# Queries and keys of dilations 1 and 4 by seven products, rotated as pairs of heads inside the pair stage

## The chip, the core and the metric

The kernel runs on one core of a Trainium2 chip. The metric is the device time of one execution in microseconds (us); fewer is better. The engines are named as in the profile: PE is TensorE (matmul), PEld its weight load, DVE is VectorE, ACT is ScalarE, POOL is GpSimd, SP is SyncE, which issues nearly all DMAs.

## The reference

A trunk of two layers on x of (1, 1024, 1024) in fp32. Layer 0 mixes with gated DeltaNet heads and short convolutions, layer 1 with HGRN2 heads and dilated sliding-window attention; each layer is followed by a SwiGLU FFN. What the change touches is the first half of layer 1's mixer:

```python
def mixer_cd(h, w_in, lower_bound, norm_g, w_out):
    hq, hf, hi, hg, sq, sk, sv = split_cols(h @ w_in, CD_SPLITS)
    f_gate = lb + (1.0 - lb) * jax.nn.sigmoid(hf)
    k_in = (1.0 - lb) * jax.nn.sigmoid(-hf)
    o_c = hgrn2_recurrence(silu(hq), k_in, hi, log(f_gate))
    sq = rope(sq.reshape(b, t, n_pat, SWA_HEADS, SWA_DH), pos)
    sk = rope(sk.reshape(b, t, n_pat, SWA_HEADS, SWA_DH), pos)
    for p, (window, dilation) in enumerate(SWA_PATTERNS):   # (128,1), (512,4), (2048,16)
        o_p, lse_p = dilated_window_attention(sq[:, :, p], sk[:, :, p], sv[:, :, p], window, dilation)

def rope(x, pos):
    x1, x2 = xf[..., :half], xf[..., half:]                 # lower and upper 64 of a head's 128 columns
    return concatenate([x1 * cos - x2 * sin, x1 * sin + x2 * cos], axis=-1)
```

There are 4 HGRN2 heads and, for each of 3 dilations, 4 attention heads, all 128 wide. `h @ w_in` has 52 column blocks of 128.

## The kernel before, in words

Every fp32 operand is split into a high and a low part (`split`, L100 to L103: a cast on ScalarE, then a subtraction on VectorE), and each product is three matmuls of 128x128 by 128x512 (`mm3`, L126 to L128: L126 to L128 are the lines on which nearly all matmuls stand). The sequence is held transposed, 128 features on the partitions, and in two halves of 512 tokens.

**Seven products.** Where two column blocks g and u of the same input are wanted, the 2x2 product (two column blocks by two halves of tokens) is made by seven products instead of eight. Class `Up` does so for the FFN, its subclass `Pairs` (L729) for pairs of column blocks of layer 1's mixer. A pair is 7 products x 4 blocks of the half contraction x 3 matmuls = 84 matmuls; the plain way is 96. `HEADS` lists the 12 pairs. ("k", p, h) is key and query of attention head h of dilation group p (0: dilation 1, 1: dilation 4, 2: dilation 16); ("f", h) is forget gate and query of HGRN2 head h. Positions in `HEADS` are counted from 0.

`pair` (and `last_pair`) is one window of the stage; the order on PE, DVE, ACT, POOL and SP is that of the code there (`manual_schedule`). In window f, PE makes p1(f), p2(f), row2(f-1), row1(f-1), p6(f), p5(f), p7(f), 12 matmuls each. Beside them the outputs of pair f-1 are finished: at the start `add22` (ACT copies x from PSUM to `c`, DVE adds z to `c`, L797), then `row2` accumulates on the same PSUM bank x and so needs that copy first; `row1` accumulates on z, and so needs DVE's total first. `add11`, `row1` and `add22` give the sums of both column blocks. In the same window the weights of pair f+1 are made: four sums on POOL (`sums`, L302 and L303; `sums_late`, L307 and L308), four splits on ACT and DVE (`part_a` to `part_d`).

What is done with an output depends on its kind. "k" is stored to DRAM (`qk`). The query of "f" is multiplied by its sigmoid (`query`, L820 and L821) and stored. For the forget gate `forget` (L828 to L840) is a generator for both halves at once: clamp on DVE, exponential and +1 on ACT, reciprocal (L836) and product (L838) on DVE, scale and shift on ACT (L840). `step()` puts its next part into the code order, at three places of a window.

**The mixer behind it.** Then come the projections of the values, gates and the rest as plain products (`hgrn_v`, `swa_v`, `hgrn_gates`), between which attention (`local`) and HGRN2 (`chain`) run. After every few matmuls the projections call `tick(cost)`; it adds cost times `rate` to what is due for the two generators and runs their next step when 1 is due. The PE order is that of the code, DVE's is fixed in these steps. Three forms of rotation are there:

- dilation 1 (`turns`, L1939): q and k are loaded from DRAM twice, once with the halves of the partitions exchanged, rotated by three DVE operations (L1935 to L1937) with a table `turn0` loaded at L1948, stored to `final`, and loaded from there by `Attend.load`.
- dilation 4 (`swa_qk`, L1966): q and k of a head are made by plain products, 96 matmuls; ACT exchanges the halves out of PSUM (L1976, L1977, tile `sw`), DVE rotates (L1980, L1981). `query_keys` calls it for each head.
- dilation 16 (`Attend.load`): loaded, exchanged by DMA and rotated when attention of that head is near; the stage of pairs has written these heads in the order of their 16 streams.

Of the kernel before, what the change touches and what calls it, by code (L numbers as in the profile page):

```python
# [54 lines left out]
def hybrid_trunk_kernel(ctx: ExitStack, tc: tile.TileContext, x_t, w_all, w_down, w_ba, vecs, c_f, c_i, c_rope, out):  # L55
# [673 lines left out]
    class Pairs(Up):  # L729

        early = True
        HEADS = (("k", 0, 0), ("k", 0, 1), ("k", 0, 2), ("f", 0), ("k", 2, 0), ("f", 1), ("k", 2, 1), ("f", 2),
                 ("k", 2, 2), ("f", 3), ("k", 2, 3), ("k", 0, 3))

        def __init__(self, left):
            self.left, self.n = left, 0
            n = len(self.HEADS)
            self.qk = {f[1:]: dr.tile([2, P, 2, HT], F32, name=f"qk{i}") for i, f in enumerate(self.HEADS) if f[0] == "k"}
# [5 lines left out]
            self.work, self.kept_f, self.coming = [], {}, {}  # L744

        def src(self, kind, f):
            f = self.HEADS[f]
            if f[0] == "k":
                return w_all[W_AT["cd", (16 if kind == "g" else 28) + f[1] * 4 + f[2]]]
            return w_all[W_AT["cd", (4 if kind == "g" else 0) + f[1]]]  # L750
# [27 lines left out]
        def fresh(self, name="d"):  # L778
            return self.right.tile([P, HT], F32, tag="d", name=name, bufs=4)

        def place(self, f, c):

            if f < 3:
                return c
            return self.scratch("fc") if self.HEADS[f][0] == "f" else self.fresh()

        def streams(self, f, dst, *srcs):

            n = (None, 4, 16)[self.HEADS[f][1]] if self.HEADS[f][0] == "k" else None
            if n is None:  # L790
                return (dst,) + srcs
            return (dst.rearrange("p (r i) -> p i r", r=n),) + tuple(s.rearrange("p (i r) -> p i r", r=n) for s in srcs)

        def total(self, f, i, half, c, y):

            if (self.HEADS[f][0], i) == ("f", 1):
                V.tensor_tensor(c, c, y, op=ADD)  # L797
                return self.query(f, half, c)
            d = self.place(f, c)
            o, a, b = self.streams(f, d, c, y)  # L800
            V.tensor_tensor(o, a, b, op=ADD)
            self.keep(f, i, half, d)

        def keep(self, f, i, half, d):
            kind = self.HEADS[f]
            if kind[0] == "k":
                dst = self.qk[kind[1:]][i]
                if kind[1] == 2 and i == 0:
                    dma(dst.rearrange("p b t -> p (b t)").rearrange("p (s b i) -> p s b i", s=16, b=2)[:, :, half],
                        d.rearrange("p (s i) -> p s i", s=16))  # L810
                else:
                    dma(dst[:, half], d)
                return
            self.kept_f[kind[1], half] = d
            if half:
                self.work.append(self.forget(kind[1]))
# [7 lines left out]
        def forget(self, h):  # L824
            cs = [self.kept_f.pop((h, half)) for half in range(NH)]
            rs = [self.scratch("fr") for _ in cs]
            for c, r in zip(cs, rs):
                V.tensor_scalar(c, c, -44.0, None, op0=MAX)  # L828
                S.activation(r, c, AF.Exp, scale=-1.0)
            yield  # L830
            for c, r in zip(cs, rs):
                S.activation(c, r, AF.Identity, bias=onec[:, 0:1])
            yield
            om, lb = self.omlb[:, h:h + 1], self.lb[:, h:h + 1]
            for half, (c, r) in enumerate(zip(cs, rs)):
                V.reciprocal(c, c)  # L836
                d = self.fresh("kk")
                V.scalar_tensor_tensor(d, r, om, c, op0=MULT, op1=MULT)  # L838
                dma(self.bkq[h, half][1], d)
                S.activation(c, c, AF.Identity, scale=om, bias=lb)  # L840
                dma(self.bkq[h, half][0], c)
                yield
# [1758 lines left out]
```

## Time and profile before

| | us |
|---|---|
| median of 3 runs | 2572.06 (2570.32 to 2573.62) |
| the profiled execution | 2570.22 |
| its span | 2568.4 |
| busy PE | 2544.8 |
| busy DVE | 1666.6 |
| busy ACT | 1034.8 |
| busy POOL | 522.6 |
| granted clock of PE, mean | 0.998 |

The profile's page and the answers of the trace are of that profiled execution. A line of instructions shows the engine, the line of the kernel, the operation, the tiles (out<-in), shapes and counts; L126 is line 126 of the kernel before. In the waits of TensorE a row says which instruction of which engine ended the wait, how long all such waits were, how many, and the longest. The stage of pairs lies from about 1186 to 1376 us of the span, the mixer with attention and HGRN2 from about 1378 to 1845 us.

### The profile page before, as it was taken

To read this page: it belongs to the slowest core of one execution; us is meant where nothing else is said; L and a number is where in the kernel's file an instruction comes from. 1 tells how busy PE (TensorE), PEld (TensorE's weight loads), DVE (VectorE), ACT (ScalarE), POOL (GpSimd) and SP (SyncE) were. 2 spreads that over 40 slices of the span, in tenths; PEclk is the share of its full clock that TensorE was granted. 3 is DMA by queue.
4 is the path that set the end of the run, shared out by engine and by line. 5 is a ranking of instruction groups with operands and counts; after the bars stand their busy time and mean duration, and the time that the engine had idled before them with its cause. 6 is when DMAs were issued, how large, how long until landed. Compare 5 with 4: busy or idle time off the path is not lost.

```text
span 2568.4 us, 37628 instructions
## 1 busy us (share of the span) xinstructions
PE 2544.8 (99%) x14124; PEld 2120.3 (83%) x14124; DVE 1666.6 (65%) x2823; ACT 1034.8 (40%) x1859; POOL 522.6 (20%) x445
## 2 busy tenths in 40 slices
PE   9999999999999999999999999999999999999998
PEld 7788888888888888887888887888878888888887
DVE  7886777585655665567665586665668565666554
ACT  5432123343333344344444455564544333334442
POOL 1110121334343300033330000000033433330001
PEclk9999999999999999999999999999999999999999
DMA  4434446424556688643336676625652455668853
GB/s 136 149 99 156 121 148 214 161 87 164 178 190 205 215 285 298 189 131 132 122 113 223 207 228 181 191 88 172 213 202 87 164 188 184 201 217 282 280 176 122
DMA packets 287447, 456.03 MB, mean 178 GB/s; under 512 B 50176, under 2 KB 142112, under 8 KB 287136
## 3 DMA queue, kind: packets, MB, share of 16 engines
q1 hardware_dynamic: 287264, 453.62, 54.2%
q8 instruction: 111, 1.82, 0.3%
q14 instruction: 72, 0.59, 0.1%
HBM read 311.36 MB, written 142.16 MB: 177 GB/s over the span
## 4 chain that ended last, share of the span: by engine, by line
PE 73%; DVE 6%; DMA 2%; ACT 1%; issue 1%; POOL 0%; SPq 0%; DVEq 0%; ACTq 0%; POOLq 0%
PE psu L126 13%; PE psu L128 13%; PE psu L127 13%; PE psg L126 5%; PE psg L128 5%; PE psg L127 5%; PE psm L128 4%; PE psm L127 4%; PE psm L126 4%; PE psm L2125 1%; DVE h L223 1%; DVE h L592 1%; PE psm L2067 1%; DMA raw<-in_dram 1%; DVE w L289 1%
## 5 line engine op out<-in xcount | busy, mean ns | idle before, releaser
L103 DVE TENSOR_TENSOR w<-raw,w 128x1024 fp32r<-128x1024 f32 (+1 forms) x321 | 383.7, 1197 | 131.3 <-ACT w L102 130.4
L102 ACT CAST w<-raw 128x1024 fp32r<-128x1024 f32 (+1 forms) x321 | 306.9, 958 | 270.1 <-PE psu L128 126.3
L126 PE MATMUL psu<-hnh,w 128*128 128x512 f32 x880 | 350.9, 399 | 2.8 <-ACT sw L1909 2.4
L128 PE MATMUL psu<-hnh,w 128*128 128x512 f32 x880 | 345.1, 392 | 1.0 <-DVE w L103 1.0
L127 PE MATMUL psu<-hnl,w 128*128 128x512 f32 x880 | 344.0, 391 | 0.5 <-DVE hnl L2374 0.5
L128 PEld LDWEIGHTS psu<-hnh,w 128*128 128x128 f32 x880 | 165.6, 188 | 37.9 <-DVE w L103 3.0
L126 PEld LDWEIGHTS psu<-hnh,w 128*128 128x128 f32 x880 | 165.8, 188 | 37.0 <-ACT sw L1909 2.5
L127 PEld LDWEIGHTS psu<-hnl,w 128*128 128x128 f32 x880 | 165.9, 189 | 34.2 <-DVE hnl L2374 1.3
L187 POOL TENSOR_TENSOR acc<-acc,sq 128x512 f32<-128x512 f32 x52 | 79.0, 1520 | 527.1 <-ACT sq L183 527.0
L302 POOL TENSOR_TENSOR ws<-raw 128x512 f32<-128x512 f32 x50 | 72.3, 1446 | 424.0 <-DMA raw<-in_dram 310.5
L103 DVE TENSOR_TENSOR w<-ws,w 128x1024 fp32r<-128x1024 f32 x47 | 60.7, 1292 | 119.6 <-ACT w L102 119.6
L103 DVE TENSOR_TENSOR hidq<-hr,hidq 128x1024 fp32r<-128x1024 f32 x72 | 82.1, 1141 | 81.3 <-ACT hidq L102 81.1
L102 ACT CAST hidq<-hr 128x1024 fp32r<-128x1024 f32 x72 | 70.3, 980 | 106.1 <-DMA hr<-ts 63.2
L126 PE MATMUL psm<-hidq,w 128*128 128x512 f32 x264 | 102.8, 389 | 0.0
L127 PE MATMUL psm<-hidq,w 128*128 128x512 f32 x264 | 102.8, 389 | 0.0
L128 PE MATMUL psm<-hidq,w 128*128 128x512 f32 x264 | 102.8, 389 | 0.0
L126 PE MATMUL psu<-hidq,w 128*128 128x512 f32 (+2 forms) x242 | 90.7, 375 | 0.0
L127 PE MATMUL psu<-hidq,w 128*128 128x512 f32 (+2 forms) x242 | 90.5, 374 | 0.0
L128 PE MATMUL psu<-hidq,w 128*128 128x512 f32 (+2 forms) x242 | 90.5, 374 | 0.0
L126 PE MATMUL psu<-t3h,w 128*128 128x512 f32 x224 | 87.3, 390 | 1.0 <-ACT u L365 1.0
L126 PE MATMUL psu<-t4h,w 128*128 128x512 f32 x224 | 87.5, 391 | 0.6 <-ACT c L372 0.6
L393 POOL TENSOR_TENSOR hid<-hid,c 128x512 f32<-128x512 f32 x44 | 61.7, 1402 | 125.8 <-ACT hid L392 103.4
(499 smaller groups left out, 6509.7 us busy)
## 6 DMA issues: line engine op xcount, KB each, us to landing
raw<-in_dram SPq DMA_DIRECT2D x227, 512.0 KB, 4.0
sd<-in_dram SPq DMA_DIRECT2D x44, 512.0 KB, 4.0
hid<-hid SPq DMA_DIRECT2D x88, 256.0 KB, 2.7
sd<-sd SPq DMA_DIRECT2D x44, 512.0 KB, 3.1
hr<-ts SPq DMA_DIRECT2D x40, 512.0 KB, 4.5
raw<-sd SPq DMA_DIRECT2D x40, 512.0 KB, 4.7
hd<-h SPq DMA_DIRECT2D x48, 256.0 KB, 3.0
h<-hd SPq DMA_DIRECT2D x48, 256.0 KB, 5.7
```

What stands on the lines that cost most here:

```text
L102: S.copy(hi, src)
L103: eng.tensor_tensor(lo, src, hi.bitcast(F32), op=SUB)
L126: T.matmul(o, lh, rh, start=first and i == 0, stop=False, **kw)
L127: T.matmul(o, lh, rl, start=False, stop=False, **kw)
L128: T.matmul(o, ll, rh, start=False, stop=last and i == n - 1, **kw)
L187: (eng or G).tensor_tensor(a, a, q, op=ADD)
L223: V.scalar_tensor_tensor(h, h, vec[:, row + k:row + k + 1], pb, op0=MULT, op1=MULT)
L289: later(lambda: V.tensor_tensor(u[:, 1, c], src[:, c], u[:, 0, c].bitcast(F32), op=SUB))
L302: G.tensor_tensor(s[:, HT:], b[:, :HT], b[:, HT:], op=ADD)
L393: G.tensor_tensor(h, h, self.c22.pop(f), op=MULT)
L592: eng.tensor_tensor(dst, x, y, op=SUB)
L2067: T.matmul(o[:, z], self.block(self.q, j, 1), self.block(self.k, j, m), start=True, stop=True)
```

## The change

The stage of pairs gets four pairs more and another order. A new kind ("r", p, i, m) is q (i = 0) or k (i = 1) of heads 2m and 2m+1 of dilation 1 (p = 0) or 4 (p = 1). The host reorders the weights' columns, so that one column block has the lower halves of the two heads and the other the upper halves: x1 and x2 of the rotation lie on the same partitions of two tiles. The rotation is then done in the stage of pairs, half of the tokens by half (`rope`): with a (lower) and b (upper),

- t1 = a cos on DVE, t2 = b sin and a = a sin on POOL,
- b = b cos, t1 - t2 and a + b on DVE, each result stored to `qk`. For p = 1 the results are written in the order of their 4 streams.

`turn_heads` puts the first line into the code order, `turned` the second. The table `rt` of cosines and sines has one buffer; `table` loads it, 512 KB for each half of a p = 0 pair, 256 KB once for a p = 1 pair. `swa_qk`, `turns`, `final` and `query_keys` are removed. `Attend.load` loads q and k of dilations 1 and 4 from `qk` in four pieces of 64 partitions; those of dilation 16 are now stored in plain order and permuted as they are rotated. `forget` works on one half at a time. The half of a weight tile that `part_d` fills has a tile of its own (`wd`, 2 buffers). The attention order is all heads of dilation 16, then 4, then 1; `swa_v` ticks in finer steps, and the rates are new.

```diff
-        HEADS = (("k", 0, 0), ("k", 0, 1), ("k", 0, 2), ("f", 0), ("k", 2, 0), ("f", 1), ("k", 2, 1), ("f", 2),
-                 ("k", 2, 2), ("f", 3), ("k", 2, 3), ("k", 0, 3))
+        HEADS = (("k", 2, 0), ("k", 2, 1), ("k", 2, 2), ("f", 0), ("r", 1, 0, 0), ("r", 0, 0, 0), ("f", 1),
+                 ("r", 1, 1, 0), ("r", 0, 1, 0), ("f", 2), ("r", 1, 0, 1), ("r", 0, 0, 1), ("f", 3),
+                 ("r", 1, 1, 1), ("r", 0, 1, 1), ("k", 2, 3))
...
+        def table(self, f, half):
+            if f < 3 or self.HEADS[f][0] != "r":
+                return
+            if self.HEADS[f][1] and half:
+                return
+            self.rt = self.right.tile([P, 2, HT], F32, tag="rt", name="rt", bufs=1)
+            if self.HEADS[f][1]:
+                dma(self.rt[:, :, 0:256], c_rope[:, :, T_LEN:T_LEN + 256])
+            else:
+                dma(self.rt, c_rope[:, :, half * HT:(half + 1) * HT])
+
+        def rope(self, f, half):
...
+            p = self.HEADS[f][1]
+            a, b = (self.held.pop((f, i, half)) for i in range(2))
+            t1, t2 = self.fresh(), self.fresh()
...
+            V.tensor_tensor(v(t1), v(a), cos, op=MULT)
+            G.tensor_tensor(v(t2), v(b), sin, op=MULT)
+            G.tensor_tensor(v(a), v(a), sin, op=MULT)
+            yield
+            V.tensor_tensor(v(b), v(b), cos, op=MULT)
...
+            V.tensor_tensor(d1, v(t1), v(t2), op=SUB)
+            dst = self.qk[self.HEADS[f][1:]]
+            dma(dst[0][:, half], o1)
+            V.tensor_tensor(d2, v(a), v(b), op=ADD)
+            dma(dst[1][:, half], o2)
...
-        def forget(self, h):
+        def forget(self, h, half, c):
+            r = self.scratch("fr")
+            V.tensor_scalar(c, c, -44.0, None, op0=MAX)
+            S.activation(r, c, AF.Exp, scale=-1.0)
+            S.activation(c, r, AF.Identity, bias=onec[:, 0:1])
             yield
...
+            V.reciprocal(c, c)
+            d = self.fresh("kk")
+            V.scalar_tensor_tensor(d, r, om, c, op0=MULT, op1=MULT)
+            dma(self.bkq[h, half][1], d)
+            yield
+            S.activation(c, c, AF.Identity, scale=om, bias=lb)
+            dma(self.bkq[h, half][0], c)
+            yield
...
@@ def pair
                 self.part_d(f, self.a)
                 self.fetch(n + 1)
+            self.turned()
+            self.table(f - 1, 0)
             self.step()
             self.p2(f, b21, psm())
...
             self.row2(f - 1, t4)
             self.part_a(n, an)
+            self.turn_heads(f - 1, 0)
             self.sums_late(an, bn, s)
             self.row1(f - 1, b22)
             self.p6(f, t2)
+            self.turned()
+            self.table(f - 1, 1)
             self.step()
             self.p5(f, t1, psg())
             self.part_b(n, s)
             self.part_c(n, bn)
+            self.turn_heads(f - 1, 1)
             self.a = an
             self.step()
             self.p7(f, t3)
...
-            due, rate = [0.0] * 2, [0.0, 0.72]
+            due, rate = [0.0] * 2, [0.0, 1.05]
...
-                ready += [(h, 2, None) for h in range(3)]
-                next(turner)
-                begun.append(1)
+                ready += [(h, p) for p in (2, 1, 0) for h in range(4)]
+                prepare()
...
                 swa_v(2, tick)
-                rate[0] = 0.5
+                rate[:] = .75, 1.0
...
-                query_keys((0,))
-                ready.append((3, 2, None))
+                rate[0] = 1.0
                 swa_v(0, tick)
-                rate[0] = 0.7
-                query_keys((1, 2, 3))
-                ready += [(h, 0, None) for h in (1, 2, 3)]
-                rate[0] = 1.05
+                rate[0] = 1.1
```

How the order of instructions moves is shown at two places. On DVE, before, in the window after that of a forget pair and on into the next: the clamps of both halves stand together, the reciprocals one window later, the first behind the last half split of the pair (`fc` is the forget gate's tile, `kk` what is stored of it, `w` weights, `c` the total that row1 waits for).

```order
L801 TENSOR_TENSOR fc<-u_10416,psg 128x512
L828 TENSOR_SCALAR fc<-fc 128x512 x2
L103 TENSOR_TENSOR w<-ws,w 128x1024
L103 TENSOR_TENSOR w<-raw,w 128x1024
L801 TENSOR_TENSOR d<-c_10606,psg 128x32x16
L103 TENSOR_TENSOR w<-raw,w 128x512
L836 RECIPROCAL fc<-fc 128x512
L838 SCALAR_TENSOR_TENSOR kk<-fr,omlb,fc 128x512
L801 TENSOR_TENSOR fc<-gt,psm 128x512
```

After, in the window of the forget pair at position 6, the rotation of the pair before it (`d<-gt,rt` to `gt<-gt,d`, then the second half's first product `d<-u,rt`) stands among the splits, and clamp, reciprocal and product of the gate's first half behind it (here the gate is in tile `gt`).

```order
L838 TENSOR_TENSOR d<-gt,rt 128x512
L800 TENSOR_TENSOR u_10148<-u_10148,psg 128x512
L842 TENSOR_TENSOR d<-d,rt 128x512
L848 TENSOR_TENSOR d<-d 128x512
L851 TENSOR_TENSOR gt<-gt,d 128x512
L871 TENSOR_SCALAR gt<-gt 128x512
L103 TENSOR_TENSOR w<-ws,w 128x1024
L103 TENSOR_TENSOR w<-raw,w 128x1024
L838 TENSOR_TENSOR d<-u_10148,rt 128x512
L876 RECIPROCAL gt<-gt 128x512
L878 SCALAR_TENSOR_TENSOR kk<-fr,omlb,gt 128x512
L800 TENSOR_TENSOR c_10359<-c_10359,psg 128x512
```

The reciprocal has moved ahead of the total `c`, the last row, and both stand behind the rotation, two of whose operations need results of POOL.

On ACT, the same place before: the exponentials of both halves (`fr`), two weight casts, +1 for both, then the copy `c` that row2 waits for.

```order
L365 COPY u_10002<-psu 128x512
L829 ACTIVATE fr<-fc 128x512 x2
L102 CAST w<-ws 128x1024
L102 CAST w<-raw 128x1024
L832 ACTIVATE fc<-fr,onec 128x512 x2
L856 COPY c_10056<-psu 128x512
L102 CAST w<-raw 128x512
```

After, exponential and +1 of one half stand together, ahead of the two casts and of the copy `c`.

```order
L365 COPY u_10728<-psu 128x512
L872 ACTIVATE fr<-gt 128x512
L873 ACTIVATE gt<-fr,onec 128x512
L102 CAST w<-ws 128x1024
L102 CAST w<-raw 128x1024
L897 COPY c_10794<-psu 128x512
L865 ACTIVATE r<-c_10794 128x512
```

The order of casts and copy is kept; in front of them stand operations that take their input from DVE's clamp, which is behind the rotation.

More of the change, by code (lines that the diff above doesn't have):

```diff
@@ L778, in fresh, with take, part @@
         def fresh(self, name="d"):
[L779 to L792, printed above, removed]
+            return self.right.tile([P, HT], F32, tag="d", name=name, bufs=6)
+        def take(self):
+            return unit()
+        def part(self, f, src, left, right, later=None, u=None):
+            if left or self.right is None:
+                return super().part(f, src, left, right, later, u)
+            u = self.right.tile([P, 2, HT], F32R, tag="wd", name="w", bufs=2)
+            if later:
+                S.copy(u[:, 0], src[:, HT:])
+                later(lambda: V.tensor_tensor(u[:, 1], src[:, HT:], u[:, 0].bitcast(F32), op=SUB))
+            else:
+                split(u[:, 0], u[:, 1], src[:, HT:])
+            self.units[f][right] = tuple(u[:, z].rearrange("p (k c) -> p k c", k=KH) for z in range(2))
         def total(self, f, i, half, c, y):
+            V.tensor_tensor(c, c, y, op=ADD)
             if (self.HEADS[f][0], i) == ("f", 1):
-                V.tensor_tensor(c, c, y, op=ADD)
                 return self.query(f, half, c)
[L799 to L802, printed above, removed]
+            self.keep(f, i, half, c)
         def keep(self, f, i, half, d):
@@ L806, in keep @@
             if kind[0] == "k":
[L807 to L812, printed above, removed]
-                return
-            self.kept_f[kind[1], half] = d
-            if half:
-                self.work.append(self.forget(kind[1]))
+                dma(self.qk[kind[1:]][i][:, half], d)
+            elif kind[0] == "r":
+                self.held[f, i, half] = d
+            else:
+                self.work.append(self.forget(kind[1], half, d))
@@ L2237, in mixer_cd @@
             lead = {}, {}, {}, (6, 7)
-            ready, late, diag, holding, combined, made, ended = [], [], [], [0], [0], [0], set()
+            ready, late, diag, combined, ended = [], [], [], [0], set()
             unit, ahead, valued, whole = [], [], set(), []
             def prepare():
-                if ready and not ahead and len(unit) // 2 + made[0] < 2:
+                if ready and not ahead and len(unit) // 2 < 2:
                     ahead.append(Attend(*ready.pop(0)))
@@ L2259, in local @@
                         prepare()
-                    holding[0] = len(ahead) + bool(now)
                     if now:
@@ L2289, in run @@
                     next(work, None)
-                    if work is hg_chain and begun:
-                        begun[0] += 1
-                        if begun[0] % 2 and made[0] <= len(coming):
-                            next(turner, None)
-            begun, coming = [], []
-            def arrived():
-                made[0] -= 1
-                ready.insert(0, coming.pop(0)[1])
+                    if work is hg_chain and not unit and ahead:
+                        ahead[0].turn(1)
             def tick(cost):
-                if coming:
-                    coming[0][0] -= cost
-                    if coming[0][0] <= 0:
-                        arrived()
                 for i in range(2):
@@ L2316, in mixer_cd @@
             tokens = (0, 1, 2), (3,), (4,), (5, 6, 7)
-            def query_keys(hs):
-                for h in hs:
-                    while len(unit) // 2 + len(ahead) + len(coming) > 1:
-                        run(loc)
-                    made[0] += 1
-                    qk = swa_qk(h, tick)
-                    coming.append([1.5, (h, 1, qk)])
             for i in range(2):
```

185 lines of the change are left out of this document (78 added, 107 removed).

## The prediction

> **What bounds the kernel now.** The page comes first, for the share of each engine; then the windows view, for the price of one matmul and for the load of the two stages that the change touches; then TensorE's waits.
>
> ```profile
> span 2568.4 us, 37628 instructions
> PE 2544.8 (99%) x14124; PEld 2120.3 (83%) x14124; DVE 1666.6 (65%) x2823; ACT 1034.8 (40%) x1859; POOL 522.6 (20%) x445
> ```
>
> TensorE is busy for 99% of the span, so it is the bound, and time goes only with matmuls or with the few places where it waits. The windows view has, for each stretch, the busy us of PE, PEld, DVE, ACT and POOL (with instructions), the granted clock, the DMA share and GB/s.
>
> ```profile
> 700.00:800.00 100.00, 100.00 (x442) 82.80 (x442) 57.39 (x80) 33.30 (x47) 35.47 (x27) 1.00 0.58 197
> 1206.00:1376.00 170.00, 168.95 (x748) 139.56 (x747) 111.58 (x96) 69.81 (x100) 49.38 (x31) 1.00 0.40 125
> 1378.00:1845.00 467.00, 461.37 (x4267) 394.31 (x4266) 299.18 (x902) 240.93 (x688) 9.99 (x11) 1.00 0.60 185
> ```
>
> The first row is pure products: 100.00 / 442 = 0.226 us for a 128x512 matmul. The second is the stage of pairs, the third the mixer behind it. In both PE has hardly a gap, VectorE (DVE) is 64 to 66% busy, and GpSimd (POOL) works in the first alone. The waits of TensorE that lie in these stages:
>
> ```profile
> PE psu L126 <- ACT sw L1909: 2.4, 1, 2.4
> PE psu L126 <- DVE k L1981: 2.1, 1, 2.1
> PE psu L126 <- ACT u L365: 1.0, 1, 1.0
> ```
>
> **Matmuls.** `swa_qk` made q and k of a dilation-4 head by 96 matmuls; its four heads are 384, all removed. Four more pairs of 7 x 4 x 3 = 84 come in, 336. So 48 fewer: 48 x 0.226 = **-10.8 us**, all on the engine that bounds. It is the one certain term.
>
> **Waits that leave with their code.** The 2.1 us belongs to `swa_qk` and goes. The 1.0 us came where the gate's work of the last forget pair (position 9, counted from 0) still ran in the last pair, position 11; the last forget pair is now at 12, the last at 15: **-3.1 us** together. The 2.4 us (a weight cast that heads ScalarE's queue while its load lands) stands in a stage whose order is new; I keep it as it is, between -4 if it goes and 0. The 4 is worked out from the clock behind it:
>
> ```profile
> 1550.00:1551.00 1.00, 0.66 (x2) 0.57 (x3) 0.93 (x4) 0.97 (x3) 0.00 (x0) 0.52 0.00 0
> 1551.00:1552.00 1.00, 1.00 (x4) 0.80 (x3) 0.08 (x1) 1.00 (x5) 0.00 (x0) 0.50 0.84 315
> 1552.00:1553.00 1.00, 1.00 (x3) 0.77 (x3) 0.46 (x1) 1.00 (x2) 0.00 (x0) 0.50 1.03 375
> 1553.00:1554.00 1.00, 1.00 (x5) 0.76 (x4) 1.00 (x2) 0.04 (x1) 0.00 (x0) 0.77 1.02 199
> 1584.00:1586.00 2.00, 1.48 (x7) 1.20 (x8) 0.38 (x1) 0.00 (x0) 0.00 (x0) 1.00 0.52 176
> ```
>
> Behind the 2.4 us the granted clock is 0.50 to 0.52 for three us and 0.77 in the fourth: (0.48 + 0.50 + 0.50 + 0.23) = about 1.7 us lost beside the wait. Behind the 2.1 us (1584 to 1586) it stays 1.00. So a long wait of TensorE costs itself and about 1.7 us more, a short one only itself.
>
> **Rotation in the pairs.** One pair lasts 84 x 0.226 = 19.0 us, a product 2.71. A rotated pair adds 8 VectorE and 4 GpSimd operations, against 4 sums on GpSimd now. All read two SBUF operands, and there the trace shows that VectorE and GpSimd do not run side by side. One line, two kinds of operand, then a place where it can be watched (start, duration):
>
> ```profile
> L821 DVE SCALAR_TENSOR_TENSOR d<-r,c x4: 801/1780/1784, 1222.4 to 1337.4; 128x512 f32<-128x512 f32 x4
> L821 DVE SCALAR_TENSOR_TENSOR d<-r,psu x4: 686/688/689, 1229.2 to 1343.4; 128x512 f32<-128x512 f32 x4
> ```
>
> ```profile
> 1257.60 1.23 DVE L103 TENSOR_TENSOR w<-ws,w 128x1024 fp32r<-128x1024 f32 x1 [1.82 <-ACT w L102]
> 1261.25 1.78 DVE L821 SCALAR_TENSOR_TENSOR d<-r,c 128x512 f32<-128x512 f32 x1 [0.70 <-ACT r L820]
> 1262.96 1.77 DVE L103 TENSOR_TENSOR w<-raw,w 128x512 fp32r<-128x512 f32 x1
> ```
>
> ```profile
> 1261.19 1.29 POOL L303 TENSOR_TENSOR ws<-ws,raw 128x512 f32<-128x512 f32 x1
> 1262.43 1.75 POOL L307 TENSOR_TENSOR raw<-raw 128x512 f32<-128x512 f32 x1
> ```
>
> With both inputs in SBUF the operation has a median of 1.78 us, with one in PSUM 0.69. The one of 1261.25 ends at 1263.03: the end of GpSimd's (1262.48) and 0.55 more; GpSimd's next takes 1.75 instead of 1.29. They take turns, whole instructions at a time. [...]
>
> So VectorE's two-SBUF work and all of GpSimd's are one queue. Its load in a window, with GpSimd at 1.25 us an operation (1262.43 less 1261.19) and VectorE as here:
>
> ```profile
> L1935 DVE TENSOR_TENSOR rs<-rs,turn 128x512 f32<-128x512 f32 x32 | 22.0, 687 | 13.1 <-DMA rs<-qk 11.7 <-issue 1.2
> L1980 DVE TENSOR_TENSOR sw<-sw,turn 128x512 f32<-128x512 f32 x16 | 11.1, 691 | 10.7 <-ACT sw L1977 10.6
> L1981 DVE TENSOR_TENSOR q<-psu,sw 128x512 f32<-128x512 f32 x8 | 8.6, 1076 | 0.1
> ```
>
> GpSimd 8 x 1.25 = 10.0. Splits of weights: three of 1.14 (1.23 less the overlap of starts) and a half one of 0.6, 4.0. The rotation 8 x 0.6 = 4.8 (0.69 less the same overlap), or, where a dilation-4 pair writes permuted (1.08), 4 x 0.6 + 4 x 1.0 = 6.4. Together 18.8 and 20.4 us of 19.0. The window without a rotation holds about 11. In a period of three pairs (57 us) it fits, so GpSimd is not a lasting bound; within it, two full windows come one behind the other, and each half's rotation is a chain with a load in it, since `rt` has one buffer:
>
> ```profile
> raw<-in_dram SPq DMA_DIRECT2D x227, 512.0 KB, 4.0
> DMA to landing us min/median/max: 5.0/5.0/5.0
> ```
>
> A load of 512 KB takes 4.0 (weights, DMA part of the page) to 5.0 us (the same cosine and sine table at L1948, by the source view); I take 4.5 to 5, from the end of the half before. On SP's queue the table's load waits for that buffer, and behind it stand the stores of the rotated halves and the next pair's weights; those are wanted a window later, so I price this at 0. On GpSimd the two late sums stand behind the rotation's products; the weights made of them are first wanted by p6 of the next window, 10.9 us after its start: 0 too.
>
> **The walk through a forget window.** VectorE and ScalarE take their work in program order. Behind the rotation stand, in the window of a forget pair (position 6), its clamp, exponential, reciprocal and product, and behind those what TensorE needs: ScalarE's copy `c` (before row2) and VectorE's total `c` (before row1). Their durations, from timelines of the same stage now:
>
> ```profile
> 1241.95 3.34 DVE L836 RECIPROCAL fc<-fc 128x512 f32<-128x512 f32 x1
> 1245.33 0.75 DVE L838 SCALAR_TENSOR_TENSOR kk<-fr,omlb,fc 128x512 f32<-128x512 f32 x1
> 1269.94 1.53 DVE L828 TENSOR_SCALAR fc<-fc 128x512 f32<-128x512 f32 x2
> ```
>
> ```profile
> 1234.46 1.15 ACT L829 ACTIVATE fr<-fc 128x512 f32<-128x512 f32 x2
> 1236.45 1.05 ACT L102 CAST w<-raw 128x1024 fp32r<-128x1024 f32 x1
> 1237.40 1.34 ACT L832 ACTIVATE fc<-fr,onec 128x512 f32<-128x512 f32 x2
> 1239.42 0.59 ACT L856 COPY c<-psu 128x512 f32<-128x512 f32 x1 [0.68 <-PE psu L128]
> ```
>
> Times from the start of window 6. The dilation-4 window before it runs about 3 us over (20.4 of load with waits for data inside); with two sums of GpSimd between, its last output is written at 9.7. The table of the dilation-1 half is issued at 10.1, lands at 14.6; two GpSimd products, four VectorE operations and two late sums taking turns end at 21.8; the clamp (0.76) at 22.5. ScalarE: exponential 0.6, identity 0.7, two casts 1.9, then the copy: ready at 26.1, where row2 is due two products into window 7, at 19.0 + 5.4 = 24.5. **Wait 1.6 us.** The second half's table lands at 27.0; GpSimd's and VectorE's first product end at 28.8, and the reciprocal stands behind it: 32.1; product 33.1 with its turn; total 0.6: 33.7. Row1 is due one product behind row2, at 26.1 + 2.7 = 28.8. **Wait 4.9 us**, and 1.7 of clock. A period costs 1.6 + 4.9 + 1.7 = 8.2, and there are three (positions 6, 9, 12; ahead of position 3 nothing is rotated): **+24.6 us**. The bounds: 0 if each step is 2 us earlier than I have it and the loads take 4.0 (the chain has two loads and four turns), 11 if the window starts another 3 us late. In the last pair the totals stand behind the second half's rotation of position 14: load at 22.0, total at 27.4 against a row1 due at 22.5: 4.9 + 1.7 = **+6.6 us**, 0 to 8.
>
> **The rest.** VectorE loses 12 operations, ScalarE 8, SP's queue 6 issues; the dilation-4 heads no longer copy halves on ScalarE, and 16 rotations with DMA exchange go. In the mixer VectorE then works at less per head, but the same attention stands beside 384 fewer matmuls, 87 of 467 us: its 64% becomes at most 299 / 380 = 79%. It still fits; I take 0, from 0 to +6 (three waits like the 2.1 us) for the newly paced steps, whose order no row of before shows. Loads of q and k in four pieces and a permuted write (1.08 for 0.69, 16 x 0.4 = 6 us of VectorE) lie under that.
>
> **Sum.** -10.8 - 3.1 + 24.6 + 6.6 = +17.3 us on the profiled run's 2570.2 (span 2568.4 and 1.8 around it), which lies 1.8 below the median of 2572.1. On the median: 2589. A measurement of this kernel can tell about 0.2%, 5.1 us, from no change.
>
> **The rivals.** *The rotation hides* (chance 0.34): windows slip by less than the two products that row2 has. Without the turns each GpSimd product runs beside VectorE, a half is shorter by some 4 us, and the walk ends about 1.9 us ahead of row1: no wait in the pairs. For it: 57 us of period against 51 of load. The total is -10.8 - 3.1 and 0 to +6: 2558 to 2564, the low end if the 2.4 us goes as well being 2554. *Half of it* (0.17): only row1 waits, 2 to 3 us, no clock loss or in one period of three: +10 to +17 of waits on -13.9, 2568 to 2575, within 0.2%. *The mixer starves*: by the third windows row VectorE has 79% and then loses its free time in the first attention heads, where permuted rotation and values meet; three waits of 2 us and two of clock give +9 on any of these cases; I count its weight into the forecast's high side (0.05 on its own, 2594 to 2602). *The saving is not there*: the pairs' 336 and the removed 384 matmuls are counted, so I give it nothing.
>
> **How the numbers follow.** Forecast 0.44 with its own range 2579 to 2598 (the period's cost between 5 and 11 us), the mixer 0.05, so slower by over 0.2%: 0.49; half 0.17; hidden 0.34. The range holds the forecast's, the half's and most of the hidden case: 2557 to 2600.
>
> **What would show it.** Right: in the profile after, TensorE's waits in the pairs name ScalarE's copy `c` and VectorE's total `c` in the windows behind positions 6, 9 and 12, 1 to 5 us each, with granted clock near 0.5 behind them; GpSimd products and VectorE's two-SBUF operations at 1.5 to 2 us; some 31 us (24.6 + 6.6) of idle TensorE and lost clock there. Wrong: the pairs' PE without gaps and clock at 1.00 (the hidden rival), waits without clock loss (half), or waits only behind the start of attention (the mixer).

## The result, and the profile after

The changed kernel takes 2603.56 us (median of 4, 2602.12 to 2604.97) against 2572.84 us beside it: ratio 1.0121, 95% interval 1.0103 to 1.0138. It is slower, as forecast, but by 31 us where 17 were forecast, and above the range's end of 2600. The page of the changed kernel and the rows of its waits of TensorE that matter:

```profile
span 2600.3 us, 37629 instructions
PE 2554.1 (98%) x14076; PEld 2127.0 (82%) x14076; DVE 1699.7 (65%) x2811; ACT 1026.6 (39%) x1851; POOL 595.2 (23%) x493
```

```profile
PE psg L126 <- DVE c L800: 14.3, 4, 5.1
PE psu L126 <- ACT c L897: 8.2, 3, 3.6
PE psm L199 <- POOL acc L187: 3.0, 1, 3.0
```

TensorE has 48 matmuls fewer and is busy 9.3 us longer, since matmuls at the low clock (granted 0.50) last longer (0.80 for 0.50 us where a wait ends, below). The two large waits are the ones that the walk named, row1 for VectorE's total `c` (L800) and row2 for ScalarE's copy `c` (L897). TensorE's timeline has them one by one (start of the matmul that waited; in brackets the wait):

```profile
1284.32 0.50 PE L126 MATMUL psu<-t4h,w 128*128 128x512 f32 x1 [1.41 <-ACT c L897]
1292.04 0.80 PE L126 MATMUL psg<-b22h,w 128*128 128x512 f32 x1 [4.71 <-DVE c L800]
1352.74 0.80 PE L126 MATMUL psu<-t4h,w 128*128 128x512 f32 x1 [3.60 <-ACT c L897]
1360.47 0.51 PE L126 MATMUL psg<-b22h,w 128*128 128x512 f32 x1 [2.24 <-DVE c L800]
1420.37 0.80 PE L126 MATMUL psu<-t4h,w 128*128 128x512 f32 x1 [3.21 <-ACT c L897]
1428.10 0.50 PE L126 MATMUL psg<-b22h,w 128*128 128x512 f32 x1 [2.24 <-DVE c L800]
1437.91 0.50 PE L126 MATMUL psu<-t3h,w 128*128 128x512 f32 x1 [1.27 <-ACT u L365]
1488.06 0.80 PE L126 MATMUL psg<-b22h,w 128*128 128x512 f32 x1 [5.09 <-DVE c L800]
1856.49 1.26 PE L2220 MATMUL psu<-cf,ol 128*128 128x128 f32 x4 [1.97 <-DVE ol L2213]
```

The forecast had 1.6 and 4.9 us in each window behind a forget pair and 4.9 in the last; the first has 1.4 and 4.7, the last 5.1. VectorE in the window of position 6, which starts at 1258.15, with what ended its waits:

```profile
1273.10 0.69 DVE L838 TENSOR_TENSOR d<-gt,rt 128x512 f32<-128x512 f32 x1 [2.91 <-DMA rt<-in_dram]
1276.67 1.77 DVE L848 TENSOR_TENSOR d<-d 128x512 f32<-128x512 f32 x1
1278.36 1.78 DVE L851 TENSOR_TENSOR gt<-gt,d 128x512 f32<-128x512 f32 x1
1280.07 0.41 DVE L871 TENSOR_SCALAR gt<-gt 128x512 f32<-128x512 f32 x1
1285.15 1.78 DVE L838 TENSOR_TENSOR d<-u,rt 128x512 f32<-128x512 f32 x1
1286.86 3.34 DVE L876 RECIPROCAL gt<-gt 128x512 f32<-128x512 f32 x1
1291.31 0.68 DVE L800 TENSOR_TENSOR c<-c,psg 128x512 f32<-128x512 f32 x1
```

The table lands 15.0 us into the window (14.6 forecast), the first half is done at 22.0 (21.8), the reciprocal ends at 32.1 (32.1), the total at 33.8 (33.7); each sum or difference of the rotation takes 1.77 us here, beside GpSimd, and 0.69 where GpSimd rests (the sum at 1294.50).

By stage, from the waits and from windows of 1 us (a "half clock" of so many us is TensorE time lost to the low clock: 1 less the granted clock, times TensorE's busy share), after less before, on spans 31.9 us apart:

| | us |
|---|---|
| 48 matmuls x 0.226 | -10.9 |
| waits in the pairs, 23.8 less 1.0 | +22.8 |
| half clock in the pairs, 11.0 less 0 | +11.0 |
| mixer: waits 5.5 less 5.0, half clock 1.6 less 1.6 | +0.5 |
| output projection and norm: waits 3.0 less 2.0, half clock 3.3 less 0 | +4.3 |
| tail: half clock 5.2 less 0 (the expectations below leave out its last 2 us and have 5.0) | +5.2 |
| other waits, ahead of the pairs and in the tail: 6.2 less 7.0 | -0.8 |
| sum | 32.1 |

### The profile page after: what moved, and what is told of

It is laid out like the page before. It is cut to its first block, busy times and chain, and to the rows that moved or that the text cites. A ratio compares the mean times of both kernels' runs of the same rounds, so it can differ in the third digit from the quotient of the medians.

```text
span 2600.3 us, 37629 instructions
## 1 busy us (share of the span) xinstructions
PE 2554.1 (98%) x14076; PEld 2127.0 (82%) x14076; DVE 1699.7 (65%) x2811; ACT 1026.6 (39%) x1851; POOL 595.2 (23%) x493
## 4 chain that ended last, share of the span: by engine, by line
PE 65%; DVE 10%; DMA 3%; issue 3%; ACT 2%; POOL 1%; SPq 0%; DVEq 0%; POOLq 0%; ACTq 0%
PE psu L126 11%; PE psu L128 11%; PE psu L127 11%; PE psg L126 5%; PE psg L128 5%; PE psg L127 5%; PE psm L126 4%; PE psm L127 4%; PE psm L128 4%; DMA rt<-in_dram 1%; DVE w L103 1%; DVE h L223 1%; PE psm L2133 1%; DVE h L592 1%; PE psm L2075 1%
## 5 line engine op out<-in xcount | busy, mean ns | idle before, releaser
L126 PE MATMUL psu<-hnh,w 128*128 128x512 f32 x832 | 330.1, 397 | 0.0
L127 PE MATMUL psu<-hnl,w 128*128 128x512 f32 x832 | 325.0, 391 | 0.4 <-DVE hnl L2350 0.4
L128 PE MATMUL psu<-hnh,w 128*128 128x512 f32 x832 | 325.4, 391 | 0.0
L128 PEld LDWEIGHTS psu<-hnh,w 128*128 128x128 f32 x832 | 156.3, 188 | 33.0 <-DVE w L103 0.3
L127 PEld LDWEIGHTS psu<-hnl,w 128*128 128x128 f32 x832 | 156.5, 188 | 32.6 <-DVE hnl L2350 1.6
L126 PEld LDWEIGHTS psu<-hnh,w 128*128 128x128 f32 x832 | 156.4, 188 | 31.6
L302 POOL TENSOR_TENSOR ws<-raw 128x512 f32<-128x512 f32 x54 | 78.9, 1462 | 414.7 <-DMA raw<-in_dram 240.5
L103 DVE TENSOR_TENSOR w<-ws,w 128x1024 fp32r<-128x1024 f32 x51 | 69.9, 1371 | 124.3 <-ACT w L102 124.1
L126 PE MATMUL psu<-t4h,w 128*128 128x512 f32 x240 | 96.2, 401 | 8.8 <-ACT c L897 8.2
L126 PE MATMUL psg<-b22h,w 128*128 128x512 f32 x216 | 87.1, 403 | 14.3 <-DVE c L800 14.3
L128 PE MATMUL psu<-t4h,w 128*128 128x512 f32 x240 | 95.5, 398 | 0.0
L127 PE MATMUL psu<-t4l,w 128*128 128x512 f32 x240 | 95.4, 398 | 0.0
L127 PE MATMUL psu<-t3l,w 128*128 128x512 f32 x240 | 93.5, 390 | 0.0
```

The costliest lines, as they stand in the source:

```text
L103: eng.tensor_tensor(lo, src, hi.bitcast(F32), op=SUB)
L126: T.matmul(o, lh, rh, start=first and i == 0, stop=False, **kw)
L127: T.matmul(o, lh, rl, start=False, stop=False, **kw)
L128: T.matmul(o, ll, rh, start=False, stop=last and i == n - 1, **kw)
L302: G.tensor_tensor(s[:, HT:], b[:, :HT], b[:, HT:], op=ADD)
```

## The experiments

**The clock behind the waits.** The theory: waits are lateness of the finishing work, and the low clock follows from TensorE standing still. If so, work put into the waits costs nothing and keeps the clock.

```diff
             self.p2(f, b21, psm())
+            if f in (7, 10, 13):
+                for _ in range(2):
+                    self.prod(self.y[f], f, "a12", b21)
```

(and the same in the last pair.)

> The p2 product is made three times instead of once in the windows behind the forget pairs at 6, 9 and 12 and in the last pair: 8 extra products of 12 matmuls, 21.8 us of TensorE work in front of row2. If the waits are lateness of ScalarE and VectorE behind the rotation (theory), TensorE works through the time it waited, the 23.8 us of waits in the pairs fall to about 2 to 4 us and the half clock behind them (11 us of TensorE time in the profile of the changed kernel) goes: 2592 to 2595 us, about 10 faster than the changed kernel. If the low clock has another cause than these waits, or the finishing work moves along with TensorE: 2604 to 2625 us.

Measured: 2595.42 us, ratio 1.0077 (1.0062 to 1.0092), 8 us below the changed kernel with 96 matmuls more, and 0.4 above the range expected. Half clock in the pairs falls from 11.0 to 2.8 us; waits fall to 11.6, not to 2 to 4, since p7 now waits for a copy of ScalarE (5.8 us). The low clock is the waits' doing. That the time came near the range is luck: in the pairs the 21.7 us of matmuls and the 20.4 us of waits and half clock that they saved about cancel, and the 8 us less come mostly from half clock that this profile does not have in the tail (5.2), and from less waiting and half clock at the norm (3.7).

**The norm before the last FFN.**

```diff
+                if self.layer:
+                    self.part_a(1, ga)
                 self.part_a(0, g0)
-                self.part_a(1, ga)
+                if not self.layer:
+                    self.part_a(1, ga)
```

> In the turn to layer 1's FFN the cast of the weight block that is loaded already stands ahead of the one whose load is late, and the square of the last half's fifth tile ahead of that late cast. If the 3.0 us wait at the norm (L199) and the half clock behind it come from the square's place behind a cast that waits for a load: wait 0.5 to 1.5 us, no half clock there, 2597 to 2600 us. If the late load itself is what counts, the wait moves to the first FFN product: 2602 to 2605 us.

Measured: 2599.32 us, ratio 1.0087 (1.0072 to 1.0103); the wait at L199 falls only to 1.9 us and the half clock stays, 3.4. The time lies in the expected range because this profile has no half clock in the tail. What stands in the changed kernel's ScalarE timeline, then in that of before, then in this run's:

```profile
1937.20 1.05 ACT L102 CAST w<-raw 128x1024 fp32r<-128x1024 f32 x1 [6.44 <-DMA raw<-in_dram]
1938.16 0.62 ACT L183 ACTIVATE sq<-h 128x512 f32<-128x512 f32 x1
```

```profile
1913.09 0.63 ACT L183 ACTIVATE sq<-h 128x512 f32<-128x512 f32 x1 [3.83 <-DVE h L1118]
1913.88 1.05 ACT L102 CAST w<-raw 128x1024 fp32r<-128x1024 f32 x1 [0.16 <-DMA raw<-in_dram]
```

```profile
1940.21 1.05 ACT L102 CAST w<-raw 128x1024 fp32r<-128x1024 f32 x1 [5.48 <-DMA raw<-in_dram]
1941.17 0.62 ACT L183 ACTIVATE sq<-h 128x512 f32<-128x512 f32 x1
```

The order of cast and square has turned round, in code that the change does not touch. The edit was to turn it back and did not: the late cast still stands ahead of the square, only the cast of the block loaded before has moved. So this run does not test whether the order makes the sum of squares late.

**What the rotation's lateness is made of.** One run without GpSimd's products, one without the table loads, one without any rotation.

```diff
-            t1, t2 = self.fresh(), self.fresh()
+            t1, t2 = self.fresh(), b
...
-            G.tensor_tensor(v(t2), v(b), sin, op=MULT)
-            G.tensor_tensor(v(a), v(a), sin, op=MULT)
```

> Leaves out the two sine products of each rotated half, which GpSimd made (so queries and keys of dilations 1 and 4 are not rotated rightly); table loads and the four VectorE operations stay. Theory (VectorE's two-SBUF operations and GpSimd's take turns, 5 us a window less in that queue): waits of row2 and row1 in the pairs fall from 22.5 to under 6 us, 2570 to 2580 us. Rival (the table load behind the previous half is what makes the rotation late): more than 12 us of them stay, 2585 to 2600 us.

Measured: 2570.01 us, ratio 0.9983 (0.9971 to 0.9994); waits in the pairs 5.2 us, half clock 0. The same product of the upper half by the cosine, in the changed kernel and in this run, from the source views (minimum, median, maximum in ns):

```profile
L842 DVE TENSOR_TENSOR d<-d,rt x8: 1208/1673/1770, 1252.7 to 1475.0; 128x512 f32<-128x512 f32 x8
```

```profile
L840 DVE TENSOR_TENSOR d<-d,rt x8: 680/683/1186, 1252.2 to 1447.8; 128x512 f32<-128x512 f32 x8
```

The second run:

```diff
-            if self.HEADS[f][1] and half:
-                return
+            if self.rt:
+                return
...
+            dma(self.rt, c_rope[:, :, half * HT:(half + 1) * HT])
```

> Loads one table once and uses it for all rotations (so most are rotated by wrong angles); all VectorE and GpSimd operations stay. By the walk of the prediction the two loads are about 9 of the chain's 33.7 us: with them gone row2 is in time and row1 at most 1 us late: waits in the pairs under 4 us, 2568 to 2576 us. Rival (the turn-taking alone makes the rotation late, loads hide): waits of 15 us and more stay, 2590 to 2603 us.

Measured: 2579.07 us, ratio 1.0015 (1.0004 to 1.0027); waits 10.8, half clock 1.7. Between the two expectations (5.2 us of this profile are half clock in the tail): without the loads 13 of the 23.8 us of waits are gone, and the turns alone still leave row1 up to 3.6 us late. The loads are needed for the full wait, as the walk had it, but do not bring all of it. Without GpSimd's products 18.6 us were gone; the two add up to more than the whole, since each is a link of one chain.

In the third, the products, sums and table loads are taken out:

```diff
             a, b = (self.held.pop((f, i, half)) for i in range(2))
+            yield
+            dst = self.qk[self.HEADS[f][1:]]
+            dma(dst[0][:, half], a)
+            dma(dst[1][:, half], b)
```

> Leaves out the rotation of dilations 1 and 4 and its tables: the outputs of the pairs are stored as they are. What is left is the saving of matmuls with the new order behind it. Theory: no wait of row2 or row1 in the pairs (0 to 2 us), so the changed kernel's 23.8 us of waits and 11 us of half clock go: 2567 to 2572 us, or 2560 where the norm's and the tail's half clock happen not to come. Rival (the new order of the pairs or the forget gate by halves makes the waits): 2585 to 2600 us.

Measured: 2566.49 us, ratio 0.9976 (0.9965 to 0.9987); waits in the pairs 0.8, half clock 0. Order and gate by halves cost nothing in the pairs by themselves; what is left is 6 us faster than before, though the norm's 3.2 us of wait and 4.7 of half clock around it are there.

**The gate's place in the queues.** Reciprocal and product later; then the whole gate later; then that with two more places mended.

```diff
-            self.step()
...
             self.table(f - 1, 0)
             self.step()
+            self.step()
```

> The third step of the window, which holds reciprocal and product of the forget gate, is moved behind the totals at the start of the next window; rotation, loads and exponential stay. Theory: row1's total no longer stands behind 4.1 us of reciprocal and product: in the three forget windows its waits of 4.7, 2.2 and 2.2 us fall to under 1.5 us together, row2's 1.4, 3.6 and 3.2 and the last pair's 5.1 stay: 2590 to 2596 us. Rival (the totals are late by the rotation alone): waits within 2 us of the changed kernel's, 2600 to 2606 us.

Measured: 2609.33 us, ratio 1.0142 (1.0124 to 1.0161), above both expectations. Row1's three waits fell to 0.5 us together, as expected, and row2's went too; in their place stand three waits of 9.4 us of p6 for the snapshot copy. ScalarE, then TensorE:

```profile
1296.47 0.81 ACT L881 ACTIVATE gt<-gt,lb,omlb 128x512 f32<-128x512 f32 x1 [9.95 <-DVE kk L878]
1297.19 0.56 ACT L338 COPY gt<-psu 128x512 f32<-128x512 f32 x1
```

```profile
1297.81 0.79 PE L126 MATMUL psu<-t2h,w 128*128 128x512 f32 x1 [9.34 <-ACT gt L338]
```

The gate's last step had come ahead of the copy on ScalarE and waits there for the reciprocal, which now is behind the whole rotation. The half that was tested held; the edit made a new wait of the same kind.

```diff
+            for _ in range(0 if half else 2):
+                yield
             r = self.scratch("fr")
-            V.tensor_scalar(c, c, -44.0, None, op0=MAX)
+            d, c = c, self.fresh()
+            V.tensor_scalar(c, d, -44.0, None, op0=MAX)
```

> The forget gate's first half starts two steps later (behind the totals of the next window, where nothing is rotated), the second half behind it, the clamp writes to another tile; all rotation and loads stay. Theory: both row2's and row1's waits in the three forget windows go (17.4 us and some 8 us of half clock), the last pair's 5.1 us stays: 2574 to 2582 us. Rival (the rotation's queue itself is too long, the gate only lies beside it): waits of more than 10 us stay in these or the next windows, 2590 to 2604 us.

Measured: 2604.60 us, ratio 1.012 (1.0103 to 1.0136), the rival's case, 0.6 us above its range: waits of 32.4 us. Again p6 waits for the snapshot copy, 7.1 us three times, now behind the exponential:

```profile
1294.36 0.63 ACT L875 ACTIVATE fr<-d 128x512 f32<-128x512 f32 x1 [7.17 <-DVE d L874]
1295.02 0.72 ACT L876 ACTIVATE d<-fr,onec 128x512 f32<-128x512 f32 x1
1295.65 0.57 ACT L338 COPY gt<-psu 128x512 f32<-128x512 f32 x1
```

```diff
-            self.turn_heads(f - 1, 1)
             while self.work:
...
             self.p7(f, t3)
-            self.turned()
             self.add22(f)
+            self.turn_heads(f - 1, 1)
+            self.turned()
```

(in the last pair, beside the edit of the norm and that of the run before.)

> Forget gate later as in the run with that name, the last pair's total ahead of the last half rotation, and the loaded weight block's cast first in the turn to layer 1's FFN. Theory: no wait over 1.5 us in the pairs or at the norm, half clock only by chance in the tail: 2562 to 2570 us, 3 to 10 us faster than the kernel before. Rival (what is moved out of one window makes the next late): 2573 us or more.

Measured: 2600.27 us, ratio 1.01 (1.0084 to 1.0117), the rival: row1's wait in the last pair went, the snapshot's three stayed (30.1 us of waits in all), and one of 4.1 us came in the output projection.

The next run keeps the last pair's edit and not the norm's, and starts the gate one step later still, behind the snapshot copy, without the yield at its end and with the new tile for the second half alone:

```diff
-            for _ in range(0 if half else 2):
+            for _ in range(0 if half else 3):
...
-            d, c = c, self.fresh()
+            d, c = c, (self.fresh() if half else c)
```

> The forget gate's first half starts three steps later, behind the snapshot copy of the next window, where nothing is rotated; no ScalarE operation that other work stands behind waits for the rotation any more, and in the last pair the total stands ahead of the last half rotation. Rotation, loads and the place of each half's first product (ahead of the total) stay. Theory (ScalarE's queue handed the rotation's lateness to TensorE in the two runs before): no wait for the snapshot copy, none for row2's copy; row1 waits 1 to 2.5 us in each of three windows for the total behind the first product, whose table has just landed: 2573 to 2582 us. Rival (the stage is too full, whatever the order): 15 us and more of waits in the pairs, 2585 to 2604 us.

Measured: 2595.30 us, ratio 1.0087 (1.007 to 1.01); the snapshot's waits are gone, row1's are 7.7 us (1.8 to 3.0 each, 1 to 2.5 expected), but row2 and p7 wait 9.9 us in the windows behind: 20.6 in all. The rival's range.

```diff
             self.part_c(n, bn)
-            self.turn_heads(f - 1, 1)
...
+            self.turn_heads(f - 2, 1)
             self.turned()
             self.table(f - 1, 0)
```

> As the run before, and the second half's rotation stands wholly behind the next window's total and half split, so no total waits for a table. Theory: under 4 us of waits in the pairs, no half clock there: 2564 to 2572 us, 0 to 8 us faster than the kernel before; the rotation costs nothing that the run without it does not have (2566.5 us). Rival (the rotation moved past the window makes the next window's sums and splits late): waits of 8 us and more, 2575 us or more.

Measured: 2586.57 us, ratio 1.0054 (1.004 to 1.0067); waits 13.9, half clock 5.8. Better than the change by 17 us, but the rival's range (5.0 us of this profile are half clock in the tail). With each of the last four orders less waiting is left: 32.4, 30.1, 20.6 and 13.9 us.

**The products on VectorE.** First in the changed kernel, then in the late order.

```diff
-            G.tensor_tensor(v(t2), v(b), sin, op=MULT)
-            G.tensor_tensor(v(a), v(a), sin, op=MULT)
+            V.tensor_tensor(v(t2), v(b), sin, op=MULT)
+            V.tensor_tensor(v(a), v(a), sin, op=MULT)
```

> The changed kernel with the two sine products of each rotated half on VectorE instead of GpSimd; orders, loads and the forget gate as in the change. Theory (one shared queue of VectorE's two-SBUF operations and GpSimd's): an operation costs 0.6 us in that queue on VectorE and 1.25 on GpSimd, so a window's load falls from 18.8 to 16.2 us and the turns of the products end, though VectorE has two operations more: waits in the pairs fall from 23.8 to 8 to 14 us, 2578 to 2590 us. Rival (no shared queue; VectorE is simply the fuller engine, and GpSimd relieves it): waits as before or longer, 2600 to 2612 us.

Measured: 2595.92 us, ratio 1.0086 (1.0067 to 1.0105). The time lies between the two, the waits (24.1 us) are the rival's: with the order of the change three products instead of one stand ahead of the total, at 1.75 to 1.78 us each beside GpSimd's sums, and row1 takes all the waiting (7 us three times), row2 none. What is less than in the changed kernel is half clock: 5.9 us in the pairs for 11.0, and none in the tail.

> The order of the run that moves the second half's rotation behind the totals, with the sine products on VectorE. Theory: the shared queue gets its 2.6 us a window back, the waits in the pairs fall from 13.9 to under 6 us with no half clock there: 2568 to 2576 us, about the kernel before. Rival (VectorE becomes the full engine, GpSimd's help was worth having): 2584 to 2595 us.

Measured: 2576.94 us, ratio 1.0008 (0.9998 to 1.0018), within 0.2% of the kernel before, 27 us below the change and 0.9 above the theory's range. Waits in the pairs 8.3 (under 6 expected), half clock 1.7; the largest left there, 3.9 us, is for a split of the mixer's first weights. With four operations a pair more on VectorE and four fewer on GpSimd the pairs lose 9.7 us less than in the run with the same order (waits 13.9 and half clock 5.8 there), and the kernel is 10 us faster. In this order the load of the shared queue counts for more than VectorE's own; in the order of the change it did not show in the waits.

```diff
-                o1, o2 = d1, d2 = t1, a
+                o1, o2 = d1, d2 = t1, self.fresh()
...
-            yield
+            for _ in range(1 + half):
+                yield
             S.activation(c, c, AF.Identity, scale=om, bias=lb)
```

(and the loop that splits `raws` ahead of `turned` in the last pair.)

> As the run with the late order on VectorE, with three places mended that its trace names: the first value weights are split ahead of the last window's first rotation (3.9 us wait), a dilation-1 result gets a tile of its own so that the snapshot behind it needs no store to land (2.5 us), and the gate's last ScalarE step stands behind the copy c (1.2 us). Theory (each wait left is one instruction queued behind another that waits): waits in the pairs fall from 8.3 to under 2.5 us, 2567 to 2573 us, 0 to 6 us faster than the kernel before. Rival (the next instruction in line then waits as long): 2575 us or more.

Measured: 2582.86 us, ratio 1.0032 (1.002 to 1.0043), the rival. The waits in the pairs are 11.5 us: the 3.9 us wait shrank to 1.4 and the other two went, but row1 waits 4.8 us, and the first value products 6.1 in all. This profiled execution is 4.6 us longer than that of the run before, and the tail's half clock, 5.3 us here and none there, is more than that; the rival is shown by the waits, not by the time. No version made here beats the kernel before with the rotation in it.

**Second profiles.** Both kernels unchanged.

> The kernel before, unchanged, for a second profile. If the norm's wait and half clock (2.1 and 3.3 us more after the change) and the tail's (5.0 us) belong to the change: again 0.9 us of wait at L199 and full clock at the norm and in the tail. If they come and go with a load that takes 3.6 or 5 us and with where the clock's periods fall: any of them can show here.

Measured: 2573.16 us, ratio 0.9999 (0.9988 to 1.0009). The profiled execution is the longest of ten (2582.12 us): 0.9 us at L199 again, but 1.7 of half clock near the norm, 4.9 in the tail, and 3.4 in the mixer, where the first profile has 1.6.

> The changed kernel, unchanged, for a second profile. The waits in the pairs are set by the order and should repeat within 0.5 us (23.8 us); the half clock in the pairs should come within 3 us of 11. At the norm: 3 us of wait and 3.3 of half clock if it belongs to the change; the tail's 5.0 us of half clock only by chance, since seven of the nine kernels with its tail that were profiled with it did not show it.

Measured: 2600.82 us, ratio 1.0102 (1.0088 to 1.0115); waits in the pairs 22.6 (1.2 less than in the first profile, 0.5 expected), half clock there 12.5, in the mixer 3.4, at the norm 3.0 and 3.4, in the tail 0. So the tail's half clock comes and goes with either kernel (five of the seventeen profiles have it, with 4.9 to 5.3 us), and is no part of the change. The norm's wait belongs to it: 0.9 us in both profiles of before, 2.6 to 3.7 us in twelve of the thirteen profiles of the changed kernel and of its variants that leave the norm's code as it is, 0.8 in the other (the first run); its half clock showed at 1.7 us with the kernel before too.

## Why the forecast fell short

The mechanism was forecast rightly; the step that failed is the price of the low clock behind the waits, and with it the terms that the forecast put at nothing behind the pairs. Term by term:

- *Matmuls, -10.8*: right. Without the rotation the kernel is 6 us faster than before, and the norm's loss lies on top.
- *Waits in the pairs, 6.5 x 3 + 4.9 = 24.4 us*: right, 22.5 at the places named and one more of 1.3 us, for `u` (L365), of the kind that the forecast let go with its code (1.0 before). The first window repeats the walk within 0.5 us a step; the later two share their waits out differently (3.6 and 2.2 for 1.6 and 4.9). Both causes that the walk chained, the turns with GpSimd and the table's load, are shown by taking one away: 5.2 and 10.8 us of waits are left. The rival of the hidden rotation needed VectorE's sums to run beside GpSimd's at 0.69 us; they took 1.77 there.
- *About 1.7 us of clock for each pair of waits, 6.8 in all*: the term of the sum that failed. Measured 11.0 and 12.5. The 1.7 came from one wait of 2.4 us behind which one period of the low clock stood (3.41 us, 1550.05 to 1553.46, at a granted clock of 0.50). The forecast had four such periods, the changed kernel has eight: in the window behind position 9 both waits brought one (from 1351.31 and 1361.55), and three times a second period followed, where 2.17, 1.43 and 0.79 us of the wait lay in the first. It was not the length that decided: the longest wait, 5.09 us, was followed by one period only, since 0.22 us of it were left when the clock fell. "A short one only itself" failed too: the same wait of 2.1 us in the mixer of the kernel before cost 1.7 us of clock in its second profile and nothing in the first.
- *Waits that leave with their code, -2.1, and the mixer at 0*: both large waits left (2.1 and 2.4), and six of 0.4 to 2.0 us stand there now; together +0.5, where -2.1 was in the sum. That VectorE would run short in the mixer, the third rival, did not show.
- *Nothing outside the stages touched*: failed. The norm's 4.3 us lie behind both stages; the forecast did not look there. An order on ScalarE turned round there, and a load was there some 5.4 us after its issue (5.0 in the second profile), where it took 3.6 in both profiles of before. With the changed order and a load of 3.6 us (the first run) the wait was 0.8, so the order alone does not make it; whether the late load would do so in the old order stays open. The half clock of the tail (5.2) is in this profile by chance, but it is not what put the time above the range: the second profile, without it, is one of 2600.9 us.

What the sum missed is so 4.2 us of clock in the pairs, 2.6 in the mixer, 4.3 at the norm and 5.2 of chance in the tail, 16.3 us, less 1.7 of smaller terms (0.6 of waits in the pairs among them); the difference of spans is 14.6 above the forecast (31.9 less 17.3).

## What to carry to other kernels

Work that was moved under matmuls was free here only where nothing that TensorE waits for stood behind it in a queue (waits in the pairs: 23.8 us with the rotation, 0.8 without it): follow each queue from the moved instruction to the next thing that a matmul needs, and again after each fix, since the wait went to the next in line (with the reciprocal later, from row1 to the snapshot copy, 9.34 us at the place shown). VectorE operations with two SBUF inputs and GpSimd operations took turns here: the product by the cosine had a median of 1.67 us with GpSimd's products beside it and 0.68 without them. A product took 1.2 us on GpSimd (L840, median) and 0.69 on VectorE. Price a stall of TensorE with its low clock, by whole periods (3.41 us at 0.50 here), and compare the order of all engines far behind the change too.

## What the runs showed of the hardware

In the changed kernel the low clock starts and ends on a grid of 3.41 us. Windows in which it starts or ends (the third figure from the end is the granted clock):

```profile
1289.00:1290.00 1.00, 0.00 (x0) 0.00 (x0) 1.00 (x1) 0.00 (x0) 0.92 (x2) 0.94 0.00 0
1296.00:1297.00 1.00, 1.00 (x4) 0.81 (x3) 1.00 (x3) 0.00 (x0) 0.00 (x0) 0.65 1.06 377
1351.00:1352.00 1.00, 0.00 (x0) 0.00 (x0) 0.71 (x1) 1.00 (x2) 0.00 (x0) 0.66 0.83 303
1426.00:1427.00 1.00, 0.00 (x0) 0.00 (x0) 0.96 (x2) 0.00 (x0) 1.00 (x2) 0.80 0.00 0
1487.00:1488.00 1.00, 0.00 (x0) 0.00 (x0) 1.00 (x3) 0.69 (x1) 0.00 (x0) 0.92 0.34 135
1856.00:1857.00 1.00, 0.51 (x2) 0.37 (x2) 1.00 (x5) 0.00 (x0) 0.00 (x0) 0.74 0.00 0
```

In the window from 1290.00 to 1291.00, all of it low, the granted clock is 0.50. So a mean of 0.94 is the low clock for the last 0.12 us, and it starts at 1289.88, and likewise at 1351.32, 1487.84 and 1856.48: 61.44, 136.52 and 368.64 us apart. It ends at 1296.70, 6.82 us on, two periods of the 3.41 us that the low clock of before lasted (1550.05 to 1553.46); the three distances are 18, 40 and 108 times 3.413 us. Waiting of 1.97 us inside one period brought the low clock (1856.48), while a period with 1.70 us of it (1426.40 to the matmul at 1428.10) kept the clock.

So the price of a wait depended on where it fell on the grid. The same wait of the kernel before, in its first profile, in its second, and the window behind the second:

```profile
1584.53 0.47 PE L126 MATMUL psu<-w,hnh 128*128 128x512 f32 x1 [2.09 <-DVE k L1981]
```

```profile
1587.93 0.72 PE L126 MATMUL psu<-w,hnh 128*128 128x512 f32 x1 [2.10 <-DVE k L1981]
1588.00:1589.00 1.00, 1.00 (x3) 0.81 (x4) 0.00 (x0) 0.00 (x0) 0.00 (x0) 0.50 0.61 176
```

In the first a period ends at 1584.18 (ten periods behind 1550.05, where the low clock of that profile starts) and divides the wait into 1.74 and 0.35 us; in the second it ends at 1587.98 and holds all 2.10. In all seventeen profiles, from 1200 to 1880 us, with the waits over 0.15 us added up by period: a period at full clock with less than 1.5 us of waiting was never followed by a low one, one with 1.91 us or more always (50 of them), and in between both came. A low period with 0.61 us or more of waiting in it was always followed by another (31), one with 0.55 or less never (56). Why the clock falls in the tail, where TensorE hardly waits, and stays low at the norm for longer than these figures say, no run shows.
